# Feed-forward's first product on fp16 parts, with scales found on the chip

## The chip, the cores and the metric

The kernel runs on one core of a Trainium2 chip. The metric is the device time of one execution in microseconds (us), the median of several runs; a profiled execution comes with it, and its trace has a row for each instruction. The engines are TensorE (PE, its weight loads PEld), VectorE (DVE), ScalarE (ACT), GpSimd (POOL), and SyncE (SP), which issues DMAs. GpSimd issues DMAs too, those that cast or accumulate on the way. Each engine works through its own instructions in order.

## The reference

Two layers over 1024 tokens of width 1024, each a pair of parallel groups (attention of eight heads on low-rank queries, keys and values; a gated convolution of 31 taps) with an output projection, and then a gated feed-forward with a convolution of 3 taps. The part that the change is about:

```python
D_MODEL, SEQ, DEPTH, D_FF = 1024, 1024, 2, 2816
...
        c_kv = _rmsnorm(p[..., o1:o2], g_kv[l])
        kv = (c_kv @ w_ukv[l].astype(h.dtype)).reshape(b, s, MLA_HEADS, MLA_NOPE_DIM + MLA_V_DIM)
        v = kv[..., MLA_NOPE_DIM:]
...
        y = jnp.concatenate([y_attn, u], axis=-1) @ w_o[l].astype(h.dtype)
        x = x + y
        h2 = _rmsnorm(x, g_ffn[l])
        z = _dwconv(h2 @ w_up[l].astype(h2.dtype), w_dw_ffn[l], b_dw_ffn[l])
        zg, zv = jnp.split(z, 2, axis=-1)
        x = x + (jax.nn.silu(zg) * zv) @ w_down[l].astype(h2.dtype)
```

The first product of the feed-forward is h2 @ w_up: 1024 tokens, 1024 inputs, 5632 outputs.

## The kernel before, in words

**Layout.** Features lie on the 128 partitions, the 1024 tokens along the free dimension, in two halves of 512 (left, right). A matrix operand is kept as two parts, a high part rounded to the short form fp32r of TensorE and a low part, the rest. A product is then three matmuls: high by high, high by low, low by high.

**The up product** (up_steps, line 1058 on). w_up is taken in NF = 22 pairs of row blocks f, one block for the gate and one for the value. For each f the two blocks, cut into halves of the inputs, make a 2 by 2 block matrix, and it is multiplied by seven products instead of eight (a Strassen form): products 1 and 2 take the gate block's halves a11 and a12 as they are, 4 takes a22, and 5, 6, 3 and 7 take sums and differences, worked out in place by combine (line 1067, four subtractions or additions). sets[i] holds the matching seven input operands b (inputs 1 and 2 are the normed halves; 5, 3, 6, 7, 4 are mixes). Each product (i, f) is 4 blocks of inputs times 3 matmuls of 128 x 128 by 512: twelve matmuls at line 1118. So each f has 84 matmuls. evict (line 1129 on) brings a bank's result to SBUF, by a copy on ScalarE or an addition on VectorE, and then the filter of 3 taps, silu and the gate's product follow.

**The weights' parts before.** Parts 1, 2 and 4 are cast by software DMAs on GpSimd's queue straight from memory (cast_pair, turn; line 190 accumulates the source to the negated high part). The blocks for the sums are fetched in f32 by SP (fetch), combined on VectorE, and split in part: a cast on ScalarE and a low part on VectorE or by such a DMA.

**Order of the work.** feed (line 898) holds a list of steps, one unit of TensorE's work each, and put(step, rank, work) hangs other work behind a step, lower ranks first. Steps 0 to 15 are the output projection (wo_steps): heads(c, i) multiplies the attention's outputs ys for half c, convs(c, i) those of the convolution, us. The order is heads(0, 0..3), heads(1, 0..2), convs(0, 0..3) as steps 7 to 10, heads(1, 3) as step 11, convs(1, 0..3) as steps 12 to 15. A step of these fills two banks po. VectorE adds them to the residual y, ScalarE squares the sums (tiles fss), VectorE adds the squares up, root(c) turns them on TensorE (rf_0t), takes the root in some small operations on VectorE, and spread(c) puts it over the partitions (rf_0s). norm and first then make the inputs b of products 1 and 2; mix (MIX_AT, steps 18 to 31) the rest. Up products begin at step 16, in the order of START (lines 90 to 92): 1 and 2 of f = 0 to 3, then (5, 0), (5, 1), (3, 0), (3, 1), (6, 0), (6, 1), (5, 2), (5, 3), (7, 0) and so on; f = 0 to 3 (LEFT = 4) go together, since the mixes aren't ready yet. From f = 4 the order is that of ORDER, f by f.

**Slots.** SBUF tiles come from pools by tag (SLOTS): 31 of 128x1024 f32 in "b" (blk), 8 in "m", 3 in "wr" (fetched blocks), 8 in "ws" (weight parts). A tile that asks for a slot gets that of an earlier one and waits for its last readers. PSUM banks go round by tag.

**The value scale.** value_squares (line 857) squares the value weights on ScalarE, value_scale (line 864) adds them up over the partitions with two small f32 matmuls (vf0p, vf1p, line 868), and VectorE makes a power of two and its inverse from the exponent. It stands where the attention begins, behind the query blocks n0 to n3 (casts at line 743). Values and the softmax's output meet as fp16 (line 1625).

**Sums for the down product** (sum_load, sum_step): rows of w_down are combined on VectorE during the up stage and stored for later.

Of the kernel before, what the change touches and what calls it, by code (L numbers as in the profile page):

```python
# [71 lines left out]
P_SCALE = 32768.0  # L72
TURNED_BY_DMA = ()
# [23 lines left out]
TAIL_STEPS = 6  # L97
ENDS = (slice(512, 768), slice(768, T))
# [27 lines left out]
class Encoder:  # L126
# [257 lines left out]
    def run(self):  # L384
# [4 lines left out]
        self.ones = self.cp.tile([128, 128], F32, name="ones")  # L389
        nc.vector.memset(self.ones, 1.0)  # L390
        self.ones_r = self.cp.tile([128, 128], F32R, name="ones_r")
# [9 lines left out]
    def first_sections(self, l, supply):  # L401
# [58 lines left out]
        nc.vector.tensor_copy(out=self.ones_r, in_=self.ones)  # L460
# [87 lines left out]
    def project(self, l, carry):  # L548
# [305 lines left out]
        return u, conv, away, (qd, qrd, kd, krd), (kvs, w["v"], self.value_squares(l, w["v"])), heads  # L854

    def value_squares(self, l, w):
        f = self.cp.tile([128, 8], F32, name=f"vf{l}", tag="vf", bufs=1)
        for k in range(2):
            t = self.blk(f"vsq{l}_{k}")[:, 0:512]
            self.nc.scalar.activation(out=t, in_=w[0][:, k * 512:(k + 1) * 512].bitcast(F32), func=AF.Square,  # L860
                                      scale=self.par[l][:, P_GKV + k:P_GKV + k + 1], accum_out=f[:, k:k + 1])
        return f

    def value_scale(self, l, f):
        nc = self.nc
        ps = self.bank(f"vf{l}p", (128, 1))
        for k in range(2):
            nc.tensor.matmul(ps, self.ones, f[:, k:k + 1], start=k == 0, stop=k == 1)
        h, s, r = (f[:, i:i + 1] for i in (2, 3, 4))
        nc.vector.tensor_scalar(out=h.bitcast(I32), in0=ps.bitcast(I32), scalar1=24, scalar2=None, op0=ALU.logical_shift_right)  # L870
        nc.vector.tensor_scalar(out=s.bitcast(I32), in0=h.bitcast(I32), scalar1=-8388608.0, scalar2=200 * 8388608.0, op0=ALU.mult, op1=ALU.add)
# [187 lines left out]
    def up_steps(self, l, steps, put):  # L1059
# [16 lines left out]
        def combine(f, o, p, q, op=ALU.subtract):  # L1076
            z = quarters(f)
            sub(z[o], z[p], z[q], op)
# [861 lines left out]
```

## Time and profile before

| what | value |
|---|---|
| median of 3 runs | 2290.26 us (2286.81 to 2290.73) |
| the profiled execution | 2288.28 us |
| its span | 2286.5 us |
| mean granted clock of TensorE | 0.997 of full speed |
| ScalarE, GpSimd busy | 57%, 34% |
| DMA: software queue, SP's queue | 48.5%, 32.8% of 16 engines' span |

The span is what the profiler's instructions cover; the execution's time is a little longer. Busy shares are means over stages. The first up stage goes from 509.6 to 930.8 us of the span, the second from 1643.1 to 2064.3. A row of a group gives the line, engine, operation, output and inputs, shapes, count, then the busy time in us, the mean in ns of one, and the engine's idle time just before, with what ended it. A row of the timeline gives the start in us, the length in us, and in brackets the idle time before and its releaser.

### The profile page before, as it was taken

What the parts mean: (1) busy time and instruction counts of PE and PEld (TensorE: products, weight loads), DVE (VectorE), ACT (ScalarE), POOL (GpSimd) and SP (SyncE); (2) the same over time, 40 slices, a digit from 0 to 9 for tenths busy, and PEclk for the clock granted to TensorE, in tenths of its full rate; (3) what the DMA queues carried; (4) which work ended last, traced back from release to release, by engine and by line L of the source; (5) the groups of instructions that cost most, each with busy time, mean ns of one, the idle gap of its engine ahead of it and who ended that gap; (6) DMA issues with size and microseconds to landing.
All of it is one profiled execution on the core that took longest, in us unless ns stands there. A gap on an engine that the chain in (4) does not pass through costs nothing.

```text
span 2286.5 us, 30445 instructions
## 1 busy us (share of the span) xinstructions
PE 2269.4 (99%) x10690; PEld 1838.8 (80%) x10690; DVE 1735.7 (76%) x2305; ACT 1298.6 (57%) x2058; POOL 781.9 (34%) x812
## 2 busy tenths in 40 slices
PE   9999999999999999999999999999999999999998
PEld 8887777788888888888888877777888888888887
DVE  7988888868877776776559778887687777768765
ACT  5355977646655555544533468785466555555444
POOL 1221788522333333001412237964323333320032
PEclk9999999999999999999999999999999999999999
DMA  6887998846899998935968979977659999988356
GB/s 195 166 181 243 193 205 180 226 133 148 211 279 293 278 295 206 334 106 143 206 137 166 224 224 205 190 157 204 175 122 228 268 303 277 293 213 316 109 120 171
DMA packets 199145, 475.73 MB, mean 208 GB/s; under 512 B 27232, under 2 KB 35280, under 8 KB 198992
## 3 DMA queue, kind: packets, MB, share of 16 engines
q0 software_dynamic: 103136, 222.46, 48.5%
q1 hardware_dynamic: 95568, 250.80, 32.8%
q8 instruction: 84, 1.38, 0.2%
q14 instruction: 69, 0.57, 0.1%
q10 hardware_dynamic: 288, 0.53, 0.1%
HBM read 309.29 MB, written 80.40 MB: 170 GB/s over the span
## 4 chain that ended last, share of the span: by engine, by line
PE 88%; DVE 6%; DMA 2%; ACT 2%; issue 2%; POOL 0%; DVEq 0%; SPq 0%; POOLq 0%; ACTq 0%
PE p L1118 34%; PE pd L1306 18%; PE po L929 7%; PE s L1562 7%; PE t L1602 4%; PE o L1625 4%; PE pa L226 2%; PE pg L226 2%; DVE conv L1777 2%; PE pg L545 2%; PE pq L226 1%; PE pv L1538 1%; PE pkv L226 1%; PE pa L545 1%; PE pn L226 1%
## 5 line engine op out<-in xcount | busy, mean ns | idle before, releaser
L1118 PE MATMUL p<-b,w 128*128 128x512 f32 x3552 | 806.9, 389 | 0.3 <-DVE w L1497 0.2
L1118 PEld LDWEIGHTS p<-b,w 128*128 128x128 f32 x3552 | 666.2, 188 | 140.3 <-DVE w L1497 1.0
L1306 PE MATMUL pd<-ab,wd 128*128 128x512 f32 (+1 forms) x1920 | 422.3, 381 | 0.0
L1306 PEld LDWEIGHTS pd<-ab,wd 128*128 128x128 f32 x1920 | 350.7, 188 | 69.5 <-DVE ab L1497 0.4
L190 POOL DMA_DIRECT2D w<-wu x96 | 84.8, 886 | 360.2 <-ACT w L189 317.7
L1562 PE MATMUL s<-k,q 96*128 96x512 f32 x768 | 207.5, 405 | 0.0
L1605 DVE SCALAR_TENSOR_TENSOR pt<-t,pt 128x512 f16<-128x512 f32 x256 | 164.8, 685 | 38.9 <-ACT pt L1604 38.3
L1794 POOL TENSOR_TENSOR late<-gate,par 128x1014 f32<-128x1014 f32 (+12 forms) x79 | 171.8, 2175 | 15.8 <-DVE qn L741 15.8
L1604 ACT ACTIVATE pt<-t 128x512 f16<-128x512 f32 x256 | 139.2, 595 | 56.6 <-PE t L1602 55.6
L1509 DVE SCALAR_TENSOR_TENSOR o<-zg,par,o 128x1023 f32<-128x1023 f32 x88 | 112.8, 1284 | 75.6 <-ACT o L1503 74.3
L190 POOL DMA_DIRECT2D w<-in_w_up x116 | 100.5, 867 | 199.4 <-ACT w L189 175.3
L1564 DVE TENSOR_REDUCE mx<-s 128x1 f32<-128x1024 f32 x128 | 155.8, 1218 | 1.2 <-PE s L1562 1.2
L1562 PEld LDWEIGHTS s<-k,q 96*128 96x128 f32 x768 | 135.4, 189 | 22.2
L1777 DVE SCALAR_TENSOR_TENSOR conv<-gate,par,conv 128x1009 f32<-128x1009 f32 (+7 forms) x112 | 142.3, 1274 | 3.7 <-ACT conv L607 1.0
L1572 ACT ACTIVATE p<-s,mx 128x1024 f32<-128x1024 f32 x128 | 143.2, 1119 | 1.8 <-DVE mx L1564 1.3
L1602 PEld LDWEIGHTS t<-ident,p 128*128 128x128 f32 x1024 | 119.8, 141 | 25.2 <-DVE yt L1632 0.8
L892 POOL DMA_DIRECT2D wd<-in_w_down x44 | 33.2, 758 | 307.7 <-PE pd L1306 301.8
L1067 DVE TENSOR_TENSOR zg<-p,zg 128x512 f32<-128x512 f32 x88 | 60.6, 690 | 99.3 <-PE p L1118 92.4
L1495 ACT CAST ab<-ac 128x512 fp32r<-128x512 f32 x130 | 80.1, 617 | 97.9 <-DVE ac L1241 95.2
L189 ACT ACTIVATE w<-w 128x512 fp32r<-128x512 f32 x212 | 133.5, 630 | 3.0
L1625 PE MATMUL o<-pt,v 128*128 128x512 f16 x512 | 132.8, 381 | 1.2 <-DVE pt L1605 1.1
L1602 PE MATMUL t<-ident,p 128*128 128x128 f32 x1024 | 133.2, 273 | 0.1
(2117 smaller groups left out, 4090.7 us busy)
## 6 DMA issues: line engine op xcount, KB each, us to landing
w<-in_w_up POOLq DMA_DIRECT2D x232, 256.0 KB, 7.2
wu<-in_w_up SPq DMA_DIRECT2D x88, 512.0 KB, 5.7
w<-wu POOLq DMA_DIRECT2D x96, 256.0 KB, 5.9
sd<-in_w_down SPq DMA_DIRECT2D x44, 512.0 KB, 9.8
ws<-sd SPq DMA_DIRECT2D x44, 512.0 KB, 6.7
wd<-in_w_down POOLq DMA_DIRECT2D x88, 256.0 KB, 5.4
act<-v SPq DMA_DIRECT2D x36, 512.0 KB, 5.8
ac<-act SPq DMA_DIRECT2D x72, 256.0 KB, 6.1
```

The source lines that it names most:

```text
L190: self.nc.gpsimd.dma_start(out=lo, in_=src, accum_op=ALU.add)
L226: nc.tensor.matmul(ps[:, HALVES[c]], w, x[:, HALVES[c]], start=(k == 0 and s == 0), stop=(k == n - 1 and s == 2))
L929: self.nc.tensor.matmul(ps, p[:, sl], q[:, cs], start=(k == 0 and t == 0), stop=(k == 3 and t == 2))
L1118: nc.tensor.matmul(ps, w[p][:, k * 128:(k + 1) * 128], b[:, q], start=(i in (1, 5, 2) and k == 0 and t == 0), stop=(k == 3 and t == 2), sk ...
L1306: nc.tensor.matmul(ps[t, m][:, cs], w[i, j][p][:, m * 128:(m + 1) * 128], b[:, q, cs], start=(i in (1, 5, 2) and j == 0 and s == 0), stop= ...
L1562: nc.tensor.matmul(ps[:, cs], q[i][0:96, qs], k[j][0:96, cs], start=(s == 0), stop=(s == 2))
L1564: nc.vector.tensor_reduce(out=mx, in_=ps, op=ALU.max, axis=AX.X, negate=True)
L1602: nc.tensor.transpose(tp[:, i, qi * 128:(qi + 1) * 128], st["p"][2 * qp + qi][:, kt * 128:(kt + 1) * 128], self.ident)
L1605: nc.vector.scalar_tensor_tensor(out=lo, in0=tp, scalar=P_SCALE, in1=hi, op0=ALU.mult, op1=ALU.subtract)
L1625: nc.tensor.matmul(po, v[2 * c + i][:, h // 2, e, :], pt[s][:, 2 * (c % 2) + i, :], start=(c == 0 and i == 0 and s == 0), stop=(c == 3 and ...
L1777: self.nc.vector.scalar_tensor_tensor(out=y[:, lo:hi], in0=u[:, lo + s:hi + s], scalar=self.tap(l, j, t), in1=y[:, lo:hi], op0=ALU.mult, o ...
L1794: self.nc.gpsimd.tensor_tensor(out=p[:, lo:hi], in0=u[:, lo + s:hi + s], in1=self.tap(l, j, t).broadcast_to([128, hi - lo]), op=ALU.mult)
```

## The change

- **fp16 parts.** All weight parts of the up product and all its seven inputs are split in two fp16 numbers (halve: a cast on ScalarE, a subtraction on GpSimd or VectorE). No weight block is cast by DMA any more; SP fetches every block in f32 (both blocks of each f, and for f = 2 and 3 a first time for products 1 and 2 and a second time for the rest).
- **Scales.** Each pair of blocks is multiplied by a power of two: ScalarE squares the blocks with a sum along the free dimension (squares), one f32 matmul with a matrix of ones adds over the partitions (total), VectorE takes the exponent and makes the power and its inverse. For f = 0 to 3 there is one total for all (first_squares in steps 5 to 10, first_total at step 11), from f = 4 one total each (own_squares, own_total). The evictions multiply by the inverse. For f = 0 to 3 the blocks are scaled in place on ScalarE (scaled); from f = 4 the scale is in the cast and in the low part's instruction.
- **GpSimd.** combine and sum_step go from VectorE to GpSimd, and so do the low parts of the weights for f = 0 to 3 and of the inputs of products 1 and 2.
- **The value scale** is found with a scale of the feed-forward's gain in one: weight_squares behind n1, scales (one small matmul of three columns, nine small operations on VectorE) behind n2.
- First total's bank: tags.insert puts it first in the round again, so that the next bank asked for (po of convs(1, 0)) is the same one.

The diff, cut to what the text speaks of:

```diff
+EXPONENT = 8388608.0
+FIRST_TOTAL = 11
...
+        scales = {1: lambda: st.update(squares=self.weight_squares(l, w["v"])),
+                  2: lambda: st.update(scale=self.scales(l, st.pop("squares")))}
         for j in range(4):
-            add(f"n{j}", f"u{j // 2}", ranked(f"u{j // 2}", j % 2, QL, f"n{j}", cqs), lambda j=j: query(j))
+            add(f"n{j}", f"u{j // 2}", ranked(f"u{j // 2}", j % 2, QL, f"n{j}", cqs), lambda j=j: query(j), scales.get(j))
...
+        ps = self.bank(f"sc{l}p", (128, 3))
+        nc.tensor.matmul(ps, self.ones, f[:, 0:3], start=True, stop=True)
...
-            sets[i].append(self.pair(x[k, 0], f"b{l}_{i}{k}", "m", True))
+            if k % 2 == 0:
+                st["two"] = self.tmp("m", f"b{l}_{i}{k}", F16, (128, 2, 2, 512))
+            sets[i].append(self.halve(st["two"][:, k % 2], x[k, 0], nc.gpsimd))
...
+        def squares(f, e, out):
+            t = self.blk(f"wsq{l}_{f}{e}")
+            nc.scalar.activation(out=t, in_=raw[f][e], func=AF.Square, accum_out=out)
+
+        def total(ps, sums, out, w):
+            nc.tensor.matmul(ps, self.ones, sums, start=True, stop=True)
+            ps = ps.rearrange("p (f e) -> p f e", e=2)
+            scale, back, v, h = (out[:, i * w:(i + 1) * w] for i in range(4))
+            nc.vector.tensor_reduce(out=v, in_=ps, op=ALU.add, axis=AX.X)
...
+        def first_total():
+            ps = self.bank(f"wt{l}", (128, 2 * LEFT))
+            tags = self.banks[1][0]
+            tags.insert(0, tags.pop())
...
+        def own_total(f):
+            t = st.pop(("sums", f))
+            ps = self.pp.tile([128, 2], F32, name=f"wt{l}_{f}", tag=f"d{6 + f % 2}", bufs=1)
+            scale[f], back[f] = total(ps, t[:, 6:8], t, 1)
+
+        def scaled(f, e):
+            nc.scalar.activation(out=raw[f][e], in_=raw[f][e], func=AF.Copy, scale=scale[f])
...
         def combine(f, o, p, q, op=ALU.subtract):
             z = quarters(f)
-            sub(z[o], z[p], z[q], op)
+            nc.gpsimd.tensor_tensor(out=z[o], in0=z[p], in1=z[q], op=op)
...
+            t, src = operand(i, f), source(i, f)
+            if f < LEFT:
+                self.halve(t, src, nc.gpsimd)
+                return
+            nc.scalar.activation(out=t[:, 0], in_=src, func=AF.Copy, scale=scale[f])
+            nc.vector.scalar_tensor_tensor(out=t[:, 1], in0=src, scalar=scale[f], in1=t[:, 0], op0=ALU.mult, op1=ALU.subtract)
...
-        for f, e, n, tag in ((0, 0, 4, "wr"), (1, 0, 5, "wr"), (0, 1, 6, "wr"), (1, 1, 9, "b"),
-                             (2, 1, 22, "b"), (2, 0, 22, "b"), (3, 0, 24, "b"), (3, 1, 24, "wr")):
-            put(n, 5, lambda f=f, e=e, tag=tag: fetch(f, e, tag))
+        for f, e, n, tag in ((0, 0, 3, "wr"), (0, 1, 4, "wr"), (1, 0, 5, "wr"), (1, 1, 6, "b"), (2, 0, 7, "b"), (3, 0, 8, "b"),
+                             (2, 1, 7, "b"), (3, 1, 8, "b"), (2, 2, 22, "b"), (2, 0, 22, "b"), (3, 0, 24, "b"), (3, 2, 24, "wr")):
+            put(n, 5, lambda f=f, e=e, tag=tag: fetch(f, min(e, 1), tag))
+            if n < 20:
+                put(n + 2, 5.5, lambda f=f, e=e: first_squares(f, e))
...
+            if n < 20 and f < 2:
+                put(FIRST_TOTAL + 1, 3.5 + f, lambda f=f, e=e: scaled(f, e))
+            elif n < 20 and e == 0:
+                put(FIRST_TOTAL + 2, 3.5 + f, lambda f=f, e=e: scaled(f, e))
+            elif n >= 20:
+                put(n + 3, 4.9, lambda f=f, e=e: scaled(f, min(e, 1)))
+        put(FIRST_TOTAL, 5.8, first_total)
+        for f in range(LEFT):
+            put(FIRST_TOTAL + 1 + f // 2, 5 + f, lambda f=f: first_part(f))
...
             for e in range(2):
-                put(n - 8, 5, lambda f=f, e=e: fetch(f, 1 - e))
...
+                put(n - 11, 5, lambda f=f, e=e: fetch(f, e, "b" if e else "wr"))
+                put(n - 8 + e, 4.5, lambda f=f, e=e: own_squares(f, e))
+            put(n - 5, 0.4, lambda f=f: own_total(f))
+            put(n - 4, 4, lambda f=f: first_part(f))
+            put(n - 3, 2, lambda f=f: (combine(f, 0, 0, 2), combine(f, 2, 2, 3, ALU.add)))
+            put(n - 2, 3, lambda f=f: part(5, f))
...
+    def halve(self, t, src, eng):
+        self.nc.scalar.copy(out=t[..., 0, :], in_=src)
+        eng.tensor_tensor(out=t[..., 1, :], in0=src, in1=t[..., 0, :], op=ALU.subtract)
+        return t
```

More of the change, by code (lines that the diff above doesn't have):

```diff
@@ L864, in value_scale @@
-    def value_scale(self, l, f):
-        nc = self.nc
[L866 to L871, printed above, removed]
-        nc.vector.tensor_scalar(out=r.bitcast(I32), in0=h.bitcast(I32), scalar1=8388608.0, scalar2=39 * 8388608.0, op0=ALU.mult, op1=ALU.add)
-        return s, r
+            nc.scalar.activation(out=t, in_=w[0][:, k * 512:(k + 1) * 512].bitcast(F32), func=AF.Square,
+                                 scale=par[:, P_GKV + k:P_GKV + k + 1], accum_out=f[:, k:k + 1])
@@ L933, in wo_steps @@
         left, right = HALVES
[L934 removed]
+        casts, ps, acc, sq, rf, us, st = {(1, m): e for m, e in casts.items()}, {}, {}, {}, {}, [], {}
         sets = self.sets = defaultdict(list)
```

176 lines of the change are left out of this document (100 added, 76 removed).

## The prediction, on record before the change was run

> **What bounds the kernel now.** I read the page first (busy shares, granted clock, chain, groups), then the waits of TensorE, then the two up stages by windows. In the fence: TensorE's share, its clock, the chain by engine, the group that the change touches, TensorE's two longest waits, and one window in the middle of the first up stage.
>
> ```profile
> PE 2269.4 (99%) x10690; PEld 1838.8 (80%) x10690; DVE 1735.7 (76%) x2305; ACT 1298.6 (57%) x2058; POOL 781.9 (34%) x812
> PEclk9999999999999999999999999999999999999999
> PE 88%; DVE 6%; DMA 2%; ACT 2%; issue 2%; POOL 0%; DVEq 0%; SPq 0%; POOLq 0%; ACTq 0%
> L1118 PE MATMUL p<-b,w 128*128 128x512 f32 x3552 | 806.9, 389 | 0.3 <-DVE w L1497 0.2
> ...
> PE vf0p L868 <- ACT vsq L860: 4.2, 1, 4.2
> PE vf1p L868 <- ACT vsq L860: 3.1, 1, 3.1
> ...
> 560.00:930.00 370.00, 369.84 (x1632) 305.74 (x1631) 270.23 (x331) 213.55 (x322) 114.39 (x151) 1.00 0.95 258
> ```
>
> TensorE is the bound: 99% busy, full clock, no wait in the up product (0.3 us over 3552 matmuls), 369.84 of 370 us busy in the window (columns: TensorE, weight loads, VectorE, ScalarE, GpSimd, then clock). Only the two value scales make it wait over 1.1 us. So two things can move the end: shorter matmuls or removed waits, and new waits, which cost their full length since nothing stands in front of TensorE to absorb them. The profiled execution took 2288.28 us, 1.98 under the median 2290.26; the sum starts from it.
>
> **1. fp16 matmuls: −41.4.** The groups of product hold 22 × 7 × 4 × 3 × 2 = 3696 matmuls (3552 of the row above and 144 on the wc tiles). Their spacing, and that of the four fp16 128x512 matmuls of the attention, from the timeline (start, length with all that are grouped):
>
> ```profile
> 597.82 52.52 PE L1118 MATMUL p<-b,w 128*128 128x512 f32 x231
> ...
> 250.43 1.04 PE L1625 MATMUL o<-pt,v 128*128 128x512 f16 x4
> 251.30 1.04 PE L1602 MATMUL t<-ident,p 128*128 128x128 f32 x8
> ...
> 253.65 1.02 PE L1625 MATMUL o<-pt,v 128*128 128x512 f16 x4
> 254.51 1.04 PE L1602 MATMUL t<-ident,p 128*128 128x128 f32 x8
> ```
>
> (52.52 − 0.389)/230 = 226.7 ns now. fp16: (251.30 − 250.43)/4 = 217.5 and (254.51 − 253.65)/4 = 215.0. I take 215.5, as the groups that follow f32 work are a little dearer at their first matmul: 3696 × 11.2 = 41.4 (bounds 3696 × 9.2 = 34 and 3696 × 11.7 = 43). The Trainium skill (TensorE: Matmul & The Clock Gate, Part 1, "Wait — 56ns, not 53.3ns?") gives N/2.4 GHz plus about 2.5 ns, 215.7 ns; by it the term would be 40.7. The fp16 row agrees within its rounding.
>
> **2. Value scale sooner: −12.** TensorE stands before vf0p, and afterwards runs at half spacing; ScalarE's queue shows why:
>
> ```profile
> 194.97 0.61 PE L226 MATMUL pn<-cqs_2l,wu10h 128*128 128x512 f32 x2
> 199.75 1.29 PE L868 MATMUL vf0p<-vf,ones 128*128 128x1 f32 x4 [4.17 <-ACT vsq L860]
> 200.90 0.77 PE L1538 MATMUL pv<-wv0h,kvs_0h 128*128 128x512 f32 x1
> ...
> 205.74 0.44 PE L1538 MATMUL pv<-wv0h,kvs_1l 128*128 128x512 f32 x1
> 206.02 0.40 PE L1538 MATMUL pv<-wv0h,kvs_0h 128*128 128x512 f32 x1
> ...
> 197.94 1.04 ACT L743 CAST qns<-qn 128x1024 fp32r<-128x1024 f32 x1 [3.54 <-DVE qn L741]
> 198.89 0.72 ACT L860 ACTIVATE vsq<-wv0h,par 128x512 f32<-128x512 f32 x1
> ```
>
> The squares (0.72 each) stand behind the cast of the last query block. After it twelve value matmuls take 206.02 − 200.90 = 5.12 instead of 12 × 0.2267 = 2.72: 2.4 lost to the clock. Layer 0 can give 4.17 + 1.15 (the four small matmuls) + 2.4 = 7.7, layer 1, with 3.1 instead of 4.2 and the rest alike, about 6.6: together 14.3. Moved between n1 and n3, the squares stand ahead of that cast, and the first value matmul waits only for evictions. What comes in is one f32 matmul with three columns for two, about 0.6 with its bubble, and half a microsecond at the next wait: 14.3 − 2 × 1.1 = 12 (bounds 8 and 14). The nine small operations on VectorE lie beside the query matmuls; without that cover they are some 1.8.
>
> **3. Totals on TensorE: +7.6.** Each of 18 f per layer, and the first four together, need one f32 matmul between products. The nearest row is the rms total, four matmuls of two passes:
>
> ```profile
> 515.06 0.95 PE L253 MATMUL rf_1p<-ones,fss 128*128 128x1 f32 x8
> 515.87 0.72 PE L1118 MATMUL p<-b,wc_1h 128*128 128x512 f32 x2
> ```
>
> 0.81/4 = 0.2 each; 38 × 0.2 = 7.6 (at 0.13 and 0.3: 5 and 11). They are not hidden, for TensorE is full.
>
> **4. Squares in the output projection: +18.3 per layer.** Here I followed the order of the changed program, engine by engine. first_squares(1, 0), step 7, takes a scratch tile of the 31 in "b". They are all in use; the slot it gets is the one of an attention output part, which the second matmul of heads(1, 3) at po_117 (step 11) reads last. ScalarE works in order, so everything behind it waits too: fss squares, the us casts, five more weight squares. VectorE's add of fss waits for ScalarE, the evictions and the us low parts wait behind it, and TensorE's turn of fss (rf_0t) waits for the last sum.
>
> ```profile
> 484.43 0.39 PE L929 MATMUL po<-ys_1l,wo 128*128 128x512 f32 x1
> 486.93 0.60 PE L265 MATMUL rf_0t<-ident,fss 128*128 128x128 f32 x4
> 487.28 0.47 PE L929 MATMUL po<-us_0h,wo 128*128 128x512 f32 x1
> 509.62 1.75 PE L1118 MATMUL p<-b,w 128*128 128x512 f32 x7
> ...
> 471.53 0.63 ACT L972 ACTIVATE fss<-y 128x512 f32<-128x512 f32 x1 [2.03 <-DVE y L967]
> 472.07 0.60 ACT L1851 CAST us_0h<-lnsg 128x512 fp32r<-128x512 f32 x1
> 472.58 0.62 ACT L1851 CAST us_1h<-lnsg 128x512 fp32r<-128x512 f32 x1
> ...
> 483.08 1.23 DVE L246 TENSOR_TENSOR fss<-fss,fss 128x1024 f32<-128x1024 f32 x1 [0.70 <-ACT fss L972]
> 484.34 0.69 DVE L979 TENSOR_TENSOR fss<-fss 128x512 f32<-128x512 f32 x1
> 487.57 0.69 DVE L276 TENSOR_REDUCE rf_0v<-rf_0t 128x4 f32<-128x512 f32 x1 [2.54 <-PE rf_0t L265]
> 489.48 0.16 DVE L281 SCALAR_TENSOR_TENSOR rf_0y<-rf_0q,rf_0y 128x4 f32<-128x4 f32 x1
> ...
> L1572 ACT ACTIVATE p<-s,mx 128x1024 f32<-128x1024 f32 x128 | 143.2, 1119 | 1.8 <-DVE mx L1564 1.3
> ```
>
> Now fss is ready at 485.0 and rf_0t starts at 486.93 without a wait. In the changed order ScalarE is let go at 484.8 (484.43 + 0.39). From there: two squares of weights (1.12 each, as L1572, the nearest with an accumulator) and four of fss (0.54): 489.3; four us casts (0.52): 491.4; two weight squares: 493.7; two of fss: 494.7; two weight squares: 497.0; the last fss squares wait for VectorE, which after 489.3 does its add (1.22), two evictions, four us low parts, an add and two evictions (0.6 each, adds 1.2): 497.2. Then 1.1 of squares, an add 1.2, the fold 0.7: **500.3 instead of 486.93, 13.4**. Behind it, po_010 takes the bank of the first weight total, and that bank's reduction stands on VectorE behind the root's chain (487.57 to 489.64, 2.07): po_010 starts 0.64 + 2.07 + 0.25 = 3.0 after rf_0t, now 0.35: 2.6 more. And after 13 us of standing TensorE starts slow as at 200.90: 2.3. Sum 18.3, so p(1, 0) moves from 509.62 to 527.9; twice 18.3 is **36.6**. Both layers have this order. Bounds: nothing, if the slot comes free earlier (rival A), otherwise 15 (cheaper squares, no slow clock) to 21 per layer.
>
> **5. GpSimd ahead of (2, 0): +2.7 per layer.** Behind the late root GpSimd has eight halves of the input and four whole first parts, and (2, 0) needs the last half. The nearest rows, a 128x512 subtraction and a 128x1024 operation:
>
> ```profile
> L1497 POOL TENSOR_TENSOR b<-y,b 128x512 fp32r<-128x512 f32 x16 | 24.2, 1626 | 28.1 <-ACT b L1495 28.1
> L1652 POOL TENSOR_TENSOR yt<-yt,rb 128x1024 f32<-128x1024 f32 x6 | 15.8, 2636 | 1.8 <-DMA rb<-sd 1.8
> ```
>
> Halves 8 × 1.63 and parts 4 × 2.64 make 23.6; from the first norm (1.4 after po_010 is through and spread, about 510.3) they reach 535 with ScalarE's casts between, where the last half would be wanted 5.0 after p(1, 0), at 532.9. That is 2 to 3.5; with 1.45 for an fp16 result it is less. I take 2.7 (0.5 to 4.5): 5.4.
>
> **6. The first fetches: +13.8 per layer.** Count from the start of p(1, 0), now 509.62. (5, 0) is at 532.80 now, at 23.2; with eight products 1.07 shorter and (2, 0) waiting 2.7 it comes at 24.8, and (5, 2), six products of 2.59 later, at 40.3. What (5, 2) needs:
>
> ```profile
> 532.80 3.56 PE L1118 MATMUL p<-b,w 128*128 128x512 f32 x15
> ...
> 537.14 1.28 DVE L1007 TENSOR_TENSOR y<-y,y 128x512 f32<-128x512 f32 x2
> ...
> 498.14 1.06 ACT L189 ACTIVATE wc_1l<-wc_1h 128x1024 fp32r<-128x1024 f32 x1
> ...
> wu<-in_w_up SPq DMA_DIRECT2D x88, 512.0 KB, 5.7
> ```
>
> VectorE has the sources of b60 at 538.42, at 28.8; in the changed order 2.2 later (the root of the right half follows (2, 0)): 31.0. Its casts, low parts, the sources of b62 and their casts (0.6 to 0.65 each, handed between the two engines): ScalarE is free at 34.7. Behind them stand the two scalings of f = 2 (1.06 each): 36.8. GpSimd then has two combines of f = 2 and the part 7 of f = 0 (3 × 1.6): 41.6. Only this last frees the weight slot into which SP fetches the second half of f = 3; it lands 5.7 later, at 47.3. GpSimd's queue has the two combines of f = 3, which wait for that load, **ahead** of the low part for (5, 2): 47.3 + 3 × 1.6 = 52.1. TensorE stands from 40.5 to 52.1, 11.6, and the slow start after it is 2.2 more: 13.8, twice **27.6**. Bounds: 5 per layer if VectorE's chain runs tighter and GpSimd's operations take 1.3, 17 if they take 2.2 (the sixteen of the row average 1.63, their pairs differ).
>
> The Trainium skill speaks against this part of the change: GPSIMD Engine Reference, "4.1 Engine selection", sends elementwise two-input work to VectorE, GpSimd being about twice as slow. By twice the 0.69 of a VectorE subtraction (L979's row) the six operations of this chain would take 1.38 each and the stall would be 1.5 shorter per layer. The row of 1626 ns says 2.4 times, and the row is what I use.
>
> **7. f from 4 on: 0.** An f needs 84 × 0.2155 = 18.1 us of TensorE. Per f ScalarE has two squares (1.12), a cast and two more operations of 128x1024 (about 1.06), five casts (0.54) and four evictions (0.58): 10.4, with the filters' starts some 12.5. VectorE, 270.23 us in the window of 370 (13.9 per 19.05), keeps its taps and low parts: 14. GpSimd has four combines and two sums, 9.8 at 1.63. All fit; parts 5, 6, 3, 7 have a step or more to spare. If one were late it would be TensorE's own wait (rival C).
>
> **Sum:** 2288.3 − 41.4 − 12 + 7.6 + 36.6 + 5.4 + 27.6 = **2312**, 1% above the median.
>
> **Rivals.**
> **A, not slower:** the squares of step 7 get a slot that is already free, or are through by 486.9, so that rf_0t keeps its place. Then the 36.6 of part 4 fall away: 2275.5. For it: ScalarE is only 57% busy. Against: the slot's last reader is a matmul of step 11 in the program's own waits. It decides from the point where ScalarE's backlog at po_117 is under 2 us.
> **B:** the second half of f = 3 lands in time for GpSimd, because part 7 of f = 0 and the scalings come 10 us sooner: without 27.6 it is 2284.5. With A as well: 2248.
> **C, much slower:** in the steady stage each own total waits, as TensorE takes it in order and its squares hang on a load of 5.7 us and ScalarE's queue. At 1.5 us in each of 36 f: 2312 + 54 = 2366. Against: fetched six steps (15.5 us) ahead of the total.
> **D, the change doesn't do what it says:** fp16 products keep 226.7 ns: 2353. Against: the rows at 250.43 and 253.65.
>
> **How the numbers follow.** Forecast 0.62 (slower, but for 0.05 of it that lies near no change), A 0.12, B 0.10 (0.06 faster, 0.04 same), A with B 0.03, C 0.10, D 0.03. A measurement of this kernel can tell about 0.2% from no change, 4.6 us around 2290.3. Faster 0.12 + 0.06 + 0.03 = 0.21; same 0.04 + 0.05 = 0.09; slower 0.70. Range: all lower bounds together give 2288.3 − 43 − 14 + 5 + 30 + 1 + 10 = 2277, all upper ones 2288.3 − 34 − 8 + 11 + 42 + 9 + 34 = 2342; with A taken in partly: 2272 to 2340.
>
> **What would show it.** Starts of the up matmuls 215 to 216 ns apart; no wait above 1 us at the value scale and no 0.43 us spacing behind it; a wait of 13 us at rf_0t with ScalarE as releaser and one of 2 to 3 at po_010; a wait of 10 us or more on GpSimd's low part at (5, 2), with a load of wu issued some 12 us before its end; no wait from f = 4 on. I am wrong if TensorE stays over 99% busy through steps 11 to 15, or if waits come in every f.

## The result, and the profile after

The changed kernel takes 2416.83 us (2416.44 to 2418.53 in 5 runs), before 2290.26; the ratio is 1.056, interval 1.0545 to 1.0574. The prediction had the direction right and the size wrong: 2312 forecast, +126.6 measured for +22. From the page after: TensorE's share, the chain by engine, the up product's group.

```profile
PE 2264.3 (94%) x10762; PEld 1517.2 (63%) x10762; DVE 1833.3 (76%) x2336; ACT 1370.3 (57%) x2124; POOL 1010.1 (42%) x784
...
PE 52%; DVE 15%; POOL 13%; issue 9%; ACT 8%; DMA 2%; POOLq 0%; SPq 0%; DVEq 0%; ACTq 0%
...
L1185 PE MATMUL p<-b,w 128*128 128x512 f16 x3696 | 831.8, 382 | 101.1 <-ACT zg L1191 43.7
```

TensorE, idle for 0.3 us in the up product before, is idle for 101.1 us there now, and only 52% of the chain that ended last runs on it (88% before). By share of the span ScalarE and VectorE are no busier than before (57% and 76%). TensorE's waits, in the view that names who was waited for (total, times, longest):

```profile
PE p L1185 <- ACT zg L1191: 43.7, 50, 1.1
PE p L1185 <- DVE zv L1192: 29.4, 34, 2.1
PE rf_0t L267 <- DVE fss L998: 24.8, 2, 12.4
PE p L1185 <- POOL w L1568: 16.2, 6, 6.9
PE rf_1s L305 <- DVE rf_1y L283: 5.0, 2, 2.5
PE po L948 <- DVE wt L1102: 4.0, 2, 2.0
PE p L1185 <- POOL b L1568: 3.0, 4, 1.3
```

The third, fourth, sixth and seventh are waits that the prediction named. The first two, 84 short ones, it did not have: TensorE waits for a PSUM bank, for ScalarE's copy of product 1 out of it ahead of product 6 (32 of the 50) or of product 6 ahead of product 7 (18), and for VectorE's addition of product 7 ahead of product 4. They come in every f of the stage but its first and its last.

By the starts of TensorE's matmuls the 128.1 us between the two spans (2286.5 and 2414.6) divide so; "over" is time beyond the count times the spacing, 226.7 ns before and 215.7 after:

| stretch | predicted | measured |
|---|---|---|
| shorter matmuls (3696 × 11.0 ns) | −41.4 | −40.7 |
| up to the projection, layer 0, layer 1 | −12 together | −2.3, −5.7 |
| projection, layer 0, layer 1 | +18.3 each | +17.1, +16.5 |
| first 28 products, over, per layer (2.0 before) | 16.5 and totals | +22.5 |
| f from 4 on, over, per layer (0 before) | 0 and 3.6 for totals | +49.1 |

The last row, 98.2 us in two layers for 7.2 forecast, holds 91 of the 104.8 us that lie between 2312 and the measured time. The 1511 matmul spacings of that stretch take 375.0 us instead of 325.9: 20.8 us per f instead of 18.1. From the start of one f's product 5 to that of the next, the f differ: f = 4 loses 5.7 us, f = 5, 6, 13, 19 and 20, which have no step of the sums for the down product beside them, lose 2.0 each on average, and the eleven f that have such steps 3.1 each.

### The profile page after: what moved, and what is told of

It reads as the page before. It is cut to its first block, busy times and chain, and to the rows that moved or that the text cites. A ratio compares the mean times of both kernels' runs of the same rounds, so it can differ in the third digit from the quotient of the medians.

```text
span 2414.6 us, 29786 instructions
## 1 busy us (share of the span) xinstructions
PE 2264.3 (94%) x10762; PEld 1517.2 (63%) x10762; DVE 1833.3 (76%) x2336; ACT 1370.3 (57%) x2124; POOL 1010.1 (42%) x784
## 4 chain that ended last, share of the span: by engine, by line
PE 52%; DVE 15%; POOL 13%; issue 9%; ACT 8%; DMA 2%; POOLq 0%; SPq 0%; DVEq 0%; ACTq 0%
PE pd L1380 17%; POOL wu L1146 8%; PE s L1641 7%; PE po L948 5%; PE t L1681 4%; PE o L1704 4%; POOL sd L1239 4%; PE p L1185 3%; DVE w L1158 2%; PE pa L228 2%; PE pg L228 2%; ACT w L1157 2%; DVE o L1588 2%; ACT wsq L1096 2%; DVE conv L1856 2%
## 5 line engine op out<-in xcount | busy, mean ns | idle before, releaser
L1185 PE MATMUL p<-b,w 128*128 128x512 f16 x3696 | 831.8, 382 | 101.1 <-ACT zg L1191 43.7
L1185 PEld LDWEIGHTS <-w 128*128 128x128 f16 x3696 | 363.0, 99 | 555.2 <-issue 123.6
L1146 POOL TENSOR_TENSOR wu<-wu,wu 128x512 f32<-128x512 f32 x132 | 179.2, 1358 | 384.1 <-DVE w L1168 307.9
L1158 DVE SCALAR_TENSOR_TENSOR w<-wu,wf,w 128x512 f16<-128x512 f32 x180 | 167.4, 930 | 167.0 <-ACT w L1157 167.0
L1157 ACT ACTIVATE w<-wu,wf 128x512 f16<-128x512 f32 x180 | 129.0, 717 | 286.9 <-POOL wu L1146 286.9
L1588 DVE SCALAR_TENSOR_TENSOR o<-zg,par,o 128x1023 f32<-128x1023 f32 x88 | 136.0, 1546 | 1.5 <-ACT o L1582 1.4
L1096 ACT ACTIVATE wsq<-wu 128x1024 f32<-128x1024 f32 x88 | 91.8, 1043 | 50.5 <-PE po L948 50.5
```

The costliest lines, as they stand in the source:

```text
L1146: nc.gpsimd.tensor_tensor(out=z[o], in0=z[p], in1=z[q], op=op)
L1157: nc.scalar.activation(out=t[:, 0], in_=src, func=AF.Copy, scale=scale[f])
L1158: nc.vector.scalar_tensor_tensor(out=t[:, 1], in0=src, scalar=scale[f], in1=t[:, 0], op0=ALU.mult, op1=ALU.subtract)
L1185: nc.tensor.matmul(ps, w[p][:, k * 128:(k + 1) * 128], b[:, q], start=(i in (1, 5, 2) and k == 0 and t == 0), stop=(k == 3 and t == 2), sk ...
L1588: self.nc.vector.scalar_tensor_tensor(out=o[:, a:b], in0=z[:, at + a:at + b], scalar=self.par[l][:, tap:tap + 1], in1=o[:, a:b], op0=ALU.m ...
```

## The experiments

Times are medians of two executions unless said otherwise. "Stage" is the stretch from f = 4 on, per layer, over 215.7 ns a matmul (over 226.7 in kernels with fp32r).

**Three first theories of the stage, and the slot.** What holds the bank copies up? T1: the way through three queues, T2: contention of VectorE and GpSimd, T3: ScalarE's load.

```diff
 combine_dve
-            nc.gpsimd.tensor_tensor(out=z[o], in0=z[p], in1=z[q], op=op)
+            (nc.gpsimd if f < LEFT else nc.vector).tensor_tensor(out=z[o], in0=z[p], in1=z[q], op=op)
```


> From f = 4 on the block sums and differences (combine) go back to VectorE; all else as in the changed kernel (2416.8 us). The changed kernel loses 49 us per layer in the stage from f = 4 on (375.0 us for 1511 matmuls, 325.9 at 215.7 ns). Theory T1 (the way VectorE low part, GpSimd combine, ScalarE cast, VectorE low part goes through three queues in order, so ScalarE stands 6 us in each f and its evictions come late): the stage falls by 35 to 45 us per layer, 2416.8 to about 2330 to 2345. Theory T2 (VectorE and GpSimd slow each other whenever both read two operands from SBUF): about half of it stays, since the sums of the down weights are still on GpSimd, 2370 to 2390. Theory T3 (ScalarE has too much work, the squares above all): within 10 us of 2416.8.

Measured 2468.6, slower by 52; stage 71.9 and 82.6. T1, T2 and T3 all missed, T1 and T2 in sign too.

```diff
 sums_dve (in sum_step)
-            add = ... nc.gpsimd.tensor_tensor
+            add = ... nc.vector.tensor_tensor
```


> Only the sums of the down weights (sum_step) go back to VectorE; the combines stay on GpSimd. T1: little, within 15 us of 2416.8, since the way through GpSimd is the same. T2: the filter taps of VectorE (L1588, 1546 ns mean for the gate's) come back towards 1284 ns, and the time falls by 30 us or more, below 2387. T3: within 10 us.

Measured 2424.9; stage 53. The gate's taps came back to 1296 ns, as T2 said, but nothing was gained, as T1 and T3 had it.

```diff
 first_part_early
-            put(n - 4, 4, lambda f=f: first_part(f))
+            put(n - 4, 2.5, lambda f=f: first_part(f))
```


> first_part (split of a11 and a12) gets rank 2.5 instead of 4 in its step, so that VectorE does its low part ahead of the filter taps; same work on every engine. T1: the combine starts some 2.6 us sooner in each f, ScalarE stands some 3.5 instead of 6 us, and 1 to 2.3 us per f go: 36 f, 2335 to 2380. T2 and T3: within 10 us of 2416.8, as no engine has less work or less overlap.

Measured 2416.1; stage 48.7. The split began some 1 us sooner, and GpSimd's first combine with it (698.98 for 699.93, in the same f); but now a tap of VectorE lay beside that combine, it took 2.25 us for 1.27, and the second began at 701.31 for 701.28. T1 in this form is out.

```diff
 squares_late
-FIRST_TOTAL = 11
+FIRST_TOTAL = 13
...
-                put(n + 2, 5.5, lambda f=f, e=e: first_squares(f, e))
+                put(max(n + 2, 11) if (f, e) != (0, 0) else n + 2, 5.5, lambda f=f, e=e: first_squares(f, e))
...
```


> The first squares behind (0, 0) come not before step 11, behind the attention heads that free their scratch slot, and the first total at step 13 instead of 11. Theory (the slot of the first squares holds ScalarE, as on record): the wait of 12.4 us at rf_0t and of 2.0 at po_010 go in both layers with the slow clock behind them, the projection falls from 115.7 to about 99 to 101 us, 2416.8 to about 2380 to 2386. Rival (the evictions or VectorE hold the root): a wait of 8 us or more stays at rf_0t, gain under 10. A loss of some us at the first products can come in with the later total.

Measured 2413.5. rf_0t still waits 9.9, since without the squares the fss tile asks for the same slot. ScalarE's row in that kernel's timeline:

```profile
480.45 2.20 ACT L991 ACTIVATE fss<-y 128x512 f32<-128x512 f32 x4 [26.29 <-PE po L948]
```

So it is not the squares' tiles that hold ScalarE but the lack of slots, whichever tile asks first. What fills them is in the diff of the change: five blocks fetched into "b" by step 8.

**Order in the queues (T4), and the two first stages.** On ScalarE two squares stand ahead of the copy that TensorE waits for, on VectorE the product of close stands ahead of the addition.

```diff
 squares_behind
-                put(n - 8 + e, 4.5, lambda f=f, e=e: own_squares(f, e))
+                put(n - 7 + e, 0.3, lambda f=f, e=e: own_squares(f, e))
 steady2: and
-            put(max(m + 3, n + 5), 3, lambda f=f: close(f))
+            put(max(m + 3, n + 5) + 1, 0.5, lambda f=f: close(f))
```


> The four runs before this left 49 us per layer in the stage from f = 4 on, whichever engine did the combines or sums and however soon the split began. TensorE's waits there are for PSUM banks: the copy of product 1's bank on ScalarE (zg, 43.7 us in 50 waits, before product 6) and the addition of product 7's on VectorE (zv, 29.4 us in 34, before product 4). Here own_squares come behind the evictions of a step (rank 0.3 of the next step instead of 4.5), same work. Theory T4 (order in the queue: two squares, 2.3 us, stand ahead of that copy): the waits for ACT zg nearly go, those for DVE zv stay; 1.3 us in each of 36 f, 2416.8 to about 2365 to 2380. Rival T5 (ScalarE and VectorE are late as a whole, through the cross-engine chain): the wait only moves to another bank, within 12 us of 2416.8.

> As squares_behind, and close (VectorE's 128x1024 product, 1.2 to 1.9 us) behind product 7's addition instead of ahead of it. T4: both waits go, the stage from f = 4 on comes to within 10 us per layer of 326 us; 2416.8 to about 2325 to 2345. T5: within 20 us of 2416.8, or the waits are for another tile.

Measured 2413.6 and 2412.1; stage 47.0 and 46.1. T4 is out. In steady2 the wait for VectorE's zv fell from 29.4 to 4.3 us, and those for ScalarE's zg and zv became 50.4 and 21.1: the wait moves to another bank and the time stays. Something else sets the pace. The chain of work in the changed kernel, one f long (start, length, what; pieces left out where they follow in the same queue):

```profile
674.45 0.17 DVE wf L1102
...
678.20 1.29 DVE w L1168
...
679.56 1.28 POOL wu L1146
...
680.90 2.14 POOL wu L1146
...
683.07 0.73 ACT w L1157
...
683.82 0.76 DVE w L1158
...
684.65 1.28 POOL wu L1146
...
685.96 0.72 ACT w L1157
686.68 0.65 ACT o L1582
...
687.71 1.13 ACT wsq L1096 x2
688.85 0.57 ACT zv L1191
689.42 0.62 ACT w L1157
...
690.07 0.78 DVE w L1158
690.85 2.21 DVE o L1588
...
694.91 0.08 DVE wf L1102
```

From one own total (wf L1102) to the next are 20.5 us, and TensorE isn't in it; from 600 to 900 us the chain has TensorE in three pieces, 9.9 us in all. I read it as a ring: VectorE's low part releases GpSimd's combine, that ScalarE's cast, that VectorE's low part, GpSimd again, and then ScalarE's and VectorE's queues go through all else that they hold until they reach the next f. VectorE and ScalarE have the time for an f's work, but not behind one another. TensorE, at 18.1 us, waits for whatever is late in it. Note the 2.14 beside 1.28 for GpSimd operations of one size, and the tap of 2.21 us (1.28 alone).

```diff
 fetch_late: first fetches of f = 2, 3 at step 11 (7 and 8), as squares_late, and
-FIRST_TOTAL = 11
+FIRST_TOTAL = 14
 (scaled and first_part of all four f at FIRST_TOTAL + 1)
```


> squares_late showed that without the squares' tiles it is the fss tile that waits for the same slot, 26.3 us: so it is the fetched blocks that fill the 31 slots. Here the four first fetches of f = 2 and 3 come at step 11 instead of 7 and 8, the squares behind (0, 0) from step 11, the first total at step 14, scaling and split at 15. Theory: rf_0t waits under 1 us, the projection falls from 115.7 to 99 to 101 us per layer; what the late total costs at the first products comes off that (up to 8 us per layer): 2416.8 to about 2384 to 2400. Rival (too few slots at any rate): a wait of over 5 us stays at rf_0t.

Measured 2397.9, in the expected range: rf_0t doesn't wait, the projection's matmuls span 98.9 us for 115.7. Some 33 us came off there in two layers; up to 4.2 us of waiting for the late scaling ahead of the first products, and their slow clock (granted 0.77 of full speed from 505 to 520 us of that trace), took back nearly half (18.9 us gained).

```diff
 fetch_b
-... (3, 0, 24, "b"), (3, 2, 24, "wr")
+... (3, 0, 24, "b"), (3, 2, 24, "b")
```


> The second block of f = 3 goes to a slot of b instead of wr, so that SP's fetch doesn't wait for GpSimd's last low part of f = 0; all else as in the changed kernel. Theory on record (that fetch makes product (5, 2) wait, 6.9 us measured with a slow clock after it): the wait for POOL w at (5, 2) falls to under 2 us in both layers, 8 to 16 us less than 2416.8. Rival (GpSimd's queue itself is behind): the wait stays within 2 us of 6.9.

Measured 2415.2 (one execution). The wait at (5, 2), in the changed kernel and here:

```profile
577.85 13.12 PE L1185 MATMUL p<-b,w 128*128 128x512 f16 x48 [6.89 <-POOL w L1568]
```
```profile
577.19 8.77 PE L1185 MATMUL p<-b,w 128*128 128x512 f16 x32 [4.37 <-POOL w L1568]
```

GpSimd waited 2.21 us for that load in the changed kernel and doesn't here, so the load held 2.5 of the 6.9 us; 4.4 are GpSimd's and ScalarE's queues themselves. That is neither the theory nor the rival; step 6 had the place and the wrong share.

**Cutting the ring (T6), and the value scale alone.**

```diff
 ring_cut
-            put(n - 4, 4, lambda f=f: first_part(f))
+            put(n - 5, 0.45, lambda f=f: first_part(f))
 ring_cut2: and the two edits of steady2
```


> T4 fell: with the copies in front the waits moved to other banks and 46 of the 49 us per layer stayed. The chain of work of the changed kernel and of steady2 from 700 to 724 us holds no TensorE at all: it goes GpSimd combine, ScalarE cast, VectorE low part, GpSimd, ScalarE (cast, filter start, copies), VectorE (low part, taps), ScalarE or VectorE, first_part's low part, and again GpSimd combine, some 20 us round. Theory T6: that is a ring from one f to the next, closed by the order in the queues, and its length, not any engine's load, is the time of an f. Here first_part comes right behind its total (step n - 5, rank 0.45, instead of n - 4, rank 4), ahead of silu on ScalarE and of the taps of the value on VectorE, which first_part_early passed only in part. T6: the ring loses taps and silu, 2.6 to 4 us, so the stage from f = 4 on falls by 30 to 45 us per layer, 2416.8 to 2325 to 2360. Rival T7 (VectorE, slowed by GpSimd, is simply full): within 15 us of 2416.8.

> ring_cut with the squares behind the evictions and close behind product 7's addition (steady2's two edits). T6: with the ring cut these two now count, the stage comes to 326 to 336 us per layer, 2416.8 to 2320 to 2345. T7: within 15 us of 2416.8.

Measured 2459.7 and 2456.2, stage 70.4 and 68.1: worse by 43 and 39. T6's forecast of this cut failed, and T7's too. GpSimd's first two combines of an f and the value's two taps on VectorE in ring_cut, and the same taps in the changed kernel:

```profile
700.63 1.71 POOL L1146 TENSOR_TENSOR wu<-wu,wu 128x512 f32<-128x512 f32 x1 [5.97 <-DVE w L1168]
702.41 2.12 POOL L1146 TENSOR_TENSOR wu<-wu 128x512 f32<-128x512 f32 x1
...
701.13 2.29 DVE L1588 SCALAR_TENSOR_TENSOR v<-zv,par,v 128x1023 f32<-128x1023 f32 x1
703.45 2.17 DVE L1588 SCALAR_TENSOR_TENSOR v<-zv,par,v 128x1023 f32<-128x1023 f32 x1
```
```profile
675.68 2.60 DVE L1588 SCALAR_TENSOR_TENSOR v<-zv,par,v 128x1023 f32<-128x1023 f32 x2
```

The first combine begins 3.1 us behind the own total, for 5.1 in the changed kernel. But now the taps of the value lie beside the combines and take 2.29 and 2.17 us, where both together took 2.60. (The tap that the expectation of all_dve below calls held back by 2.06 us is the second of them; it is stretched like the first.) So the third combine, which needs VectorE's next low part, begins 11.3 us behind the total instead of 10.2: the taps were stretched by more than the cut had gained. The ring is there again, longer.

```diff
 value_alone (the kernel before, with)
+        scales = {1: lambda: st.update(squares=self.value_squares(l, w["v"])),
+                  2: lambda: st.update(scale=self.value_scale(l, st.pop("squares")))}
```


> The kernel before with one part of the change alone: the value scale's squares behind n1, its sum behind n2. On record -12 us for both layers; in the changed kernel the attention ended 2.3 us sooner in layer 0 and the like stretch 5.7 us shorter in layer 1. As measured there: 2290 to about 2282. As on record: 2278. If in layer 0 VectorE's operations on the query blocks are slowed by GpSimd there too (two of 6.03 us for 2.36), a wait for qn of 2 to 3 us appears before the first scores.

Measured 2277.1 (4 executions; ratio 0.9953, interval 0.9937 to 0.997): 11.2 us; by the two traces 5.0 in layer 0 and 6.6 in layer 1, at their last score matmuls. The two query operations on VectorE take 4.05 us for 2.36 there, and no wait for qn shows. It is the one version here that is faster than both kernels.

**VectorE's load, contention, and the totals apart.**

```diff
 all_dve: combine_dve and sums_dve together
 no_total
-                put(n - 8 + e, 4.5, lambda f=f, e=e: own_squares(f, e))
-            put(n - 5, 0.4, lambda f=f: own_total(f))
+            put(n - 5, 0.4, lambda f=f: (scale.update({f: scale[0]}), back.update({f: back[0]})))
 all_dve_no_total: all of these
 before_pool: the kernel before, combine and sum_step on nc.gpsimd
```


> From f = 4 on both the combines and the sums go back to VectorE, so GpSimd has no two-operand work beside VectorE there. ring_cut's chain showed VectorE's own instructions stretched wherever GpSimd works (a tap 2.21 us for 1.28, a low part 1.68 for 0.74, a tap held back 2.06). Theory T8 (these stretched instructions, 4 to 5 us in each f, are what makes the ring longer than TensorE's 18.1 us): the stage from f = 4 on falls to 326 to 345 us per layer, 2416.8 to 2320 to 2360, lower than both combine_dve (2468.6) and sums_dve (2424.9). Rival T7 (VectorE is full; its own work is what counts): VectorE gets 4 us more per f, above 2460, as combine_dve was.

> As the changed kernel, but every f from 4 on takes the scale of f = 0 to 3: its squares and its total are left out. ScalarE has 2.3 us less per f, the ring loses the two squares and the total's small operations. T6 (length of the ring): 1.5 to 3 us less in each f, 2416.8 to 2310 to 2365. T7: VectorE loses 0.8 us per f, 2416.8 to about 2385 to 2395.

> Both edits: no two-operand work of GpSimd and no totals from f = 4 on (they are left out). T8 and T6: the stage within 12 us per layer of 326 us, 2320 to 2345. T7: VectorE's work per f is 17 us or more, the stage stays above 345, 2380 or more.

| time (stage over, per layer) | totals kept | totals left out |
|---|---|---|
| combines and sums on GpSimd | 2416.8 (49.1) | 2378.9 (29.8) |
| combines and sums on VectorE | 2414.8 (47.6) | 2344.8 (14.3) |

Neither single theory holds. Taking GpSimd away alone gives 1.5 us per layer, taking the totals away alone 19.3, both 34.8. no_total fell between its two forecasts, all_dve on neither, all_dve_no_total at the edge of the first. Busy time in the same 200 us (TensorE, weight loads, VectorE, ScalarE, GpSimd, clock), of the changed kernel, all_dve, no_total and all_dve_no_total:

```profile
700.00:900.00 200.00, 177.80 (x818) 80.03 (x817) 149.09 (x168) 112.44 (x160) 114.98 (x74) 1.00 0.42 159
```
```profile
700.00:900.00 200.00, 177.62 (x817) 80.28 (x815) 171.24 (x243) 115.61 (x164) 0.00 (x0) 0.99 0.45 162
```
```profile
700.00:900.00 200.00, 181.33 (x828) 80.73 (x827) 161.79 (x138) 98.64 (x129) 117.15 (x76) 1.00 0.45 171
```
```profile
700.00:900.00 200.00, 193.67 (x893) 86.96 (x892) 185.23 (x230) 108.12 (x138) 0.00 (x0) 1.00 0.50 182
```

With the sums and combines on VectorE it holds its normal durations (taps 1296 and 1279 ns) and has 171 us of work in 200; in the last kernel 185, 93%. I read it so: the work fits on neither side. Beside GpSimd VectorE's instructions stretch and the ring goes round by a third queue; on VectorE there is little slack left for any wait for ScalarE, and the squares and the total bring such waits.

> The kernel before with one part of the change alone: combine and the down weights' sums on GpSimd, all products in fp32r. VectorE has 4 us less work per f of 19.05. T8: VectorE's two-operand instructions still grow where GpSimd works (taps from 1284 ns to 1400 or more), and if the low parts wait for GpSimd it is slower, 2290 to 2310 up to 2400. T7: not slower than 2292, since VectorE has less to do.

Measured 2406.8: **119 us for moving the combines and sums alone**, without fp16 and without totals, with less work on VectorE. T7 is out as the whole cause. The stage is over by 48.3, nearly the 49.1 of the changed kernel, but it isn't lost in the same way. GpSimd's queue here issues the casting DMAs of the weights too, which the changed kernel doesn't have. The same 200 us as above, and TensorE's largest wait in total:

```profile
700.00:900.00 200.00, 180.40 (x754) 146.35 (x755) 118.24 (x88) 94.61 (x143) 157.74 (x139) 0.96 0.89 245
...
PE p L1118 <- DVE zv L1067: 63.1, 24, 4.0
```

GpSimd is busy for 157.74 us instead of 114.98, and in the stage TensorE waits for the addition of product 7 alone. How much of the 119 us is due to these DMAs in the queue was not tried.

**The two halves of that.**

```diff
 before_sums: before_pool with combine on VectorE
 before_combine: before_pool with sum_step on VectorE
```


> The kernel before with only the down weights' sums on GpSimd. No product of the up stage reads these sums, so no chain to TensorE's operands gets longer; VectorE has 88 operations of 0.69 us less. Theory T8 (the two engines hold each other up at two-operand instructions): taps and products beside the sums take 2 us and more for 1.28, and if VectorE has slack for that the time stays at 2288 to 2296; if not, more. Theory T6 (the ring of queues): 2284 to 2292.

> The kernel before with only the combines on GpSimd. T6: the way combine, cast, low part, combine through three queues is what before_pool lost by, so most of its 119 us comes here: 2370 to 2400. T8: the loss goes with the amount of overlap, combines and sums 144 to 72 operations in the f from 4 on, so about two thirds: 2350 to 2375, and before_sums has the rest.

Measured 2295.6 (7 executions; ratio 1.0034, 1.0022 to 1.0046) and 2319.9: +7.1 and +31.5 against 2288.5 beside them, 38.6 together, where both at once cost 119. The stage is over by 3.7, by 4.6, and by 48.3 with both; the first 28 products lose less than 0.1, 11.4 and 10.7 us per layer more than before. So most of before_combine's 31.5 lies in the first products. VectorE's taps (gate o, value v) of the kernel before, before_sums, before_combine and before_pool:

```profile
L1509 DVE SCALAR_TENSOR_TENSOR o<-zg,par,o 128x1023 f32<-128x1023 f32 x88 | 112.8, 1284 | 75.6 <-ACT o L1503 74.3
L1509 DVE SCALAR_TENSOR_TENSOR v<-zv,par,v 128x1023 f32<-128x1023 f32 x88 | 112.5, 1280 | 10.1 <-ACT v L1503 10.1
```
```profile
L1510 DVE SCALAR_TENSOR_TENSOR v<-zv,par,v 128x1023 f32<-128x1023 f32 x88 | 143.4, 1631 | 10.1 <-ACT v L1504 10.1
L1510 DVE SCALAR_TENSOR_TENSOR o<-zg,par,o 128x1023 f32<-128x1023 f32 x88 | 139.4, 1586 | 94.4 <-ACT o L1504 93.1
```
```profile
L1510 DVE SCALAR_TENSOR_TENSOR v<-zv,par,v 128x1023 f32<-128x1023 f32 x88 | 175.9, 2000 | 16.1 <-ACT v L1504 15.6
L1510 DVE SCALAR_TENSOR_TENSOR o<-zg,par,o 128x1023 f32<-128x1023 f32 x88 | 118.1, 1344 | 73.7 <-ACT o L1504 72.3
```
```profile
L1510 DVE SCALAR_TENSOR_TENSOR v<-zv,par,v 128x1023 f32<-128x1023 f32 x88 | 172.3, 1960 | 19.7 <-ACT v L1504 18.5
L1510 DVE SCALAR_TENSOR_TENSOR o<-zg,par,o 128x1023 f32<-128x1023 f32 x88 | 145.5, 1656 | 85.2 <-ACT o L1504 83.9
```

Both parts stretch VectorE's instructions, the sums both taps by 0.3, the combines the value's by 0.7. Either alone the stage still absorbs (under 5 us of 342.5). Both together it does not. My forecasts for before_combine, by T6 and by T8, were both too high: I divided a loss that isn't a sum. That a ring costs nothing until it is longer than TensorE's time for an f, and then all that is added to it, would explain it; this is argued from the numbers, not shown by a run of its own.

The traces also say in which f the time is lost. In us over TensorE's time for an f (84 times 215.7 or 226.7 ns), from the start of product 5 to that of the next f, mean of two layers:

| kernel | f = 4 | each f without steps of the sums | each f with them |
|---|---|---|---|
| changed | 5.7 | 2.0 | 3.1 |
| no_total | 4.7 | 0.0 | 2.3 |
| all_dve | 5.4 | 1.7 | 3.1 |
| all_dve_no_total | 4.6 | 0.1 | 0.9 |
| before_pool | 4.5 | 0.0 | 4.0 |
| before_combine | 4.7 | 0.0 | 0.0 |
| before_sums | 0.0 | 0.0 | 0.3 |

In the f without sums the own squares and totals are the whole loss: without them TensorE keeps its pace though the combines are still on GpSimd. In the f with sums it takes both away, the totals and GpSimd's operations, to come from 3.1 to 0.9. And before_pool loses nothing in an f without sums, which the changed kernel does.

> The changed kernel with all that was found taken back at once, fp16 parts kept: combines and sums on VectorE and no totals from f = 4 on (left out), first fetches of f = 2 and 3 late, second fetch of f = 3 in b. If the losses add up: 2344.8 - 18.9 - 1.7 = 2324. It can't come under 2288 by this, as the stage from f = 4 on still has 14 us per layer and the first products 20.

Measured 2320.1 for 2324: these losses lie in different stretches of the kernel, and they add up. It stays 1.4% above the kernel before (ratio 1.014, 1.011 to 1.0169).

## Why the prediction was wrong, point by point

1. **fp16 matmuls: right.** 215.7 ns a spacing in an undisturbed run of 36 (7.93 us), −40.7 for −41.4. The Trainium skill's figure (TensorE: Matmul & The Clock Gate, Part 1, "Wait — 56ns, not 53.3ns?") agrees with it: 215.7 ns.
2. **Value scale: right mechanism, a third too big in this kernel.** Alone it gave 11.2 of 12. In the changed kernel 8.0, because layer 0 kept 2.3 only. VectorE's two last-but-one query operations, before and after, and the wait that followed:

```profile
194.42 2.36 DVE L745 SCALAR_TENSOR_TENSOR qn<-qn,qns 128x1024 fp32r<-128x1024 f32 x2
...
199.02 1.94 DVE L745 SCALAR_TENSOR_TENSOR qn<-qn,qns 128x1024 fp32r<-128x1024 f32 x1 [1.11 <-ACT qns L743]
```
```profile
196.13 6.03 DVE L746 SCALAR_TENSOR_TENSOR qn<-qn,qns 128x1024 fp32r<-128x1024 f32 x2
...
203.35 2.46 PE L1641 MATMUL s<-k,q 96*128 96x512 f32 x6 [2.86 <-DVE qn L742]
```

   They take 6.03 instead of 2.36, as GpSimd's convolution taps now start beside them (196.04). The row at 199.02 stood in the trace of before, 1.94 us for an operation of 1.2: the sign of what was to come, and I didn't read it.
3. **Totals: too big on TensorE**, 0.14 us each, 5.3 for 7.6. What the own squares and totals cost by way of ScalarE's and VectorE's queues had no term: without them the kernel is 38.0 us faster in all (no_total).
4. **Squares in the projection: right in place and nearly in size**, 12.4 for 13.4 at rf_0t (released by VectorE's sum of the squares, not by ScalarE itself), 2.0 for 2.6 at po_010, 17.1 and 16.5 for 18.3. The reason was half the story: squares_late and fetch_late show that the fetched blocks take the slots.
5. **(2, 0): half as much**, 1.5 us of waiting for 2.7; GpSimd's halves took 1405 ns for the 1630 taken (the 1.45 us that step 5 names for an fp16 result stands in no row of the kernel before).
6. **First fetches: right product, wait 6.9 for 11.6**, and only 2.5 of it the load (fetch_b). GpSimd's combines there took 1.26 to 1.27 us, 1.8 times VectorE's 0.69, where I took 1.6. A second wait that I hadn't priced, 2.5 us at rf_1s, and smaller ones bring the first 28 products to 22.5 for 16.5 and totals.
7. **f from 4 on: this step failed.** "All fit": the sum has 0 here, and only the totals' own 7.2 us, where 98.2 were lost. I compared each engine's busy time with TensorE's 18.1 us, and they do fit. Two things were left out. VectorE's 13.9 us per f was taken at durations measured beside a GpSimd that issued DMAs; beside a GpSimd that works on two operands they grow. And a sum of busy times says nothing of three queues that wait for one another in turn. What the runs show in its place: the combines and sums on GpSimd and the own squares and totals lose 34.8 of the 49.1 us per layer together. Taking the first back alone gives 1.5, the second alone 19.3. The 119 us of before_pool show that the move to GpSimd can cost this much by itself, but they are no share of the 126.6: in the changed kernel the move back gains 2 us with the totals and 34 without them. That a ring of waiting queues is the reason is read from the chains; the runs that were to shorten it by order alone (first_part_early, steady2, ring_cut) gained under 5 us or lost 43. The prediction's own sign of being wrong, waits in every f, is what came.

Rival C had the right stage and a little over half the size (1.5 us an f for 2.7), but a wait that is hardly there: TensorE waited for squares at a total twice, 2.9 us in all. What stays open: the 14.3 us per layer of all_dve_no_total, 4.6 of them in f = 4 and nearly all the rest in the eleven f with sums (VectorE is at 93%; the chain also has a load of 5.2 us in it, not tried apart), the first 28 products' loss by its parts, and the length of each ring by its parts.

## What to carry to other kernels

Where an engine that was idle takes over work from a busy one, don't compare busy shares: follow one round of the loop through all the queues, from an instruction to the same one in the next round, and compare its length with the bound's time per round. Price the work that stays at durations measured beside the kind of work that will run there. And when a part taken back alone gives nothing, take back two at a time before the theory is given up: here one part gave 1.5 us per layer alone, and 15.5 where the other was out already.

## What the runs showed of the hardware

VectorE and GpSimd hold each other up. A VectorE tap of two SBUF operands takes 1.21 to 1.28 us alone and 2.21 beside a GpSimd subtraction; a 128x512 low part 0.66 and 1.68; GpSimd's 128x512 operation 1.28 and 2.14. VectorE's operation on a PSUM bank beside them doesn't grow (L1192: 745 ns in the changed kernel, where one at 699.77 lies beside the combine of 699.93, and in all_dve). The Trainium skill (SBUF — State Buffer, "Who interferes with whom") says that a VectorE instruction with two SBUF inputs contends with a GpSimd instruction that reads SBUF, and calls the pair of ports that they share an exclusive lock. These rows agree: the two combines and two taps of ring_cut end at 702.34, 703.42, 704.53 and 705.62, by turns and 1.1 us apart. The prediction had no term for it; in the kernel before GpSimd had little two-operand work beside VectorE in the up stage.
